# One hybrid gMLP/MLA step: the prompt tile's statistics on two engines, its keys last, and the eighth tile's rope queries turned during the attention

## The chip, the cores and the metric

One NeuronCore of a Trainium2 chip runs the whole program in one launch. The metric is device time in microseconds (us). Before the change three runs took 627.07, 629.03 and 629.16 us; the median is 629.03 us. Engines are called as in the profile: PE (TensorE), ACT (ScalarE), DVE (VectorE), POOL (GpSimd), SP (SyncE, which issues most of the DMAs).

## The reference

One layer over 1024 latent tokens and 128 prompt tokens, width 1024:

- h = rmsnorm(x) * (1 + scale) + shift, with scale and shift from a conditioning vector; z = h @ w_in, split into u, v, gate A (512 each), c_q (256), c_kv (128), k_rope (64), gate B (512).
- Group A mixes v over 128 positions and multiplies by gelu(u) and silu(gate A).
- Group B is latent attention with 4 heads: q = rmsnorm(c_q) @ w_uq gives per head 128 plain and 64 rope columns; ckv = rmsnorm(c_kv). The latent queries see all 1024 latent keys (rope turned by position) and 256 cached keys (queries and keys not turned) in one softmax; the prompt's 128 queries see the prompt's keys alone.
- y = concat(A, attention * silu(gate B)) @ w_o, x + gate * y, and a last rmsnorm. ckv and k_rope of the prompt are outputs too.

## The kernel before, in words

The 1152 tokens are nine tiles of 128: tiles 0 to 7 are latent, tile 8 (`NS`) is the prompt. Every large product is done in three float32r products of a high and a low part (`passes3`, L154): each PSUM result is copied rounded by ACT (the high part), and DVE subtracts that copy from the PSUM result (`lo_of`, L110, the low part). So a PE result comes back to PE by way of ACT and then DVE.

The text that the change touches is the stretch between the last input projection and the first heads of the attention:

1. **z tiles** (L1074 to L1088). For each tile t, 24 products (`z_chunk`, L1055) make c_q, c_kv and k_rope in one PSUM bank `zacc`. Between the chunks of tile t stand products for earlier tiles: `q_rope(t-2)`, `cq_transpose(t-1)`, `fold(t-1)`, `q_rope_T(t-3)` and some `q_nope`. `merged` (L211) puts them between the chunks by their cost numbers. After the last chunk, `z_stats` copies the bank to SBUF (`zs`), squares c_q and c_kv for their norms, takes roots, and scales the key (`kvn`).
2. **set-up** (L1089 to L1124). PE turns the keys (`keys`: `kT00`, `kT01` for tiles 0 to 3, `kT40`, `kT41` for 4 to 7, one for the plain, one for the rope part), the prompt's c_q (`cqT8`), the rope queries of tiles 6, 7 and 8 (`qrT`), makes the prompt's rope queries (`qr8`) and the plain queries of the third group of tiles (`qn20` to `qn23`), and turns the prompt's keys (`kT8`).
3. **attention**. A head (t, h) has three score steps on PE: two of five 128x512 products (`s1` banks, `lat`) and one of five 128x256 products (`s2`, `con`). DVE takes the row maximum, ACT the exponentials, DVE the reciprocal, POOL scales the 1280 columns (`e`). `value_steps` then turns `e` in five steps (`pT`, four transposes each), ACT copies each (`ph`), DVE makes the rest (`pl`), and PE multiplies with the values (`o`). The prompt's own small attention (`own_steps`) has four PE steps: scores, `pT8`, `o8`, and `at8` (L1401), the product with `wuv`. In pass c of the loop at L1472 the scores of heads 2c+2 and 2c+3 are merged with the values of the pair before.

The order is written by the program: `later(dt, fn)` puts an ACT, DVE or POOL instruction that much planned time behind its PE step, `run` adds the step's cost to the planned time, and `need` pulls forward what a step must have. Each engine then works through its list strictly in that order, whatever the real times are. Banks come from two pools: `pst` with 2 banks (tag `t`: `pT`, `at`, `cqT`, folds) and `psa` with 6 (tag `acc`, until the attention opens). A new tile in a pool waits until the last reader of the tile that had its bank is done: with two `pst` banks, the third `t` tile in a row waits for the readers of the first. `pss` and `pso`, which take `psa`'s banks, hold the scores and the outputs.

Of the kernel before, what the change touches and what calls it, by code (L numbers as in the profile page):

```python
# [18 lines left out]
P = 128  # L19
NT = 9  # L20
# [73 lines left out]
def tile_hymba_step(ctx: ExitStack, tc: tile.TileContext, I, O):  # L94
# [805 lines left out]
    def z_stats(t, ps):  # L900
# [9 lines left out]

        def scales():
# [41 lines left out]
        later(0.35, squares)  # L953
        later(0.9, rope_key)
        later(1.5, scales)

    def cq_transpose(t):
        last = t == NT - 1
        ps = (psa if last else pst).tile([P, 512], F32, tag="acc" if last else "t", name=f"cqT{t}")
        for q in range(2):  # L960
            T.transpose(ps[:, q * P : (q + 1) * P], zt[t][:, q * P : (q + 1) * P], ident)
        src = ps[:, 0:256].rearrange("p (q c) -> p q c", q=2)
        dh = cqh[:, :, t * P : (t + 1) * P]

        def low():
            lo_of(cql[:, :, t * P : (t + 1) * P], src, dh)
            made.add(("cq", t))

        later(0.4, lambda: S.copy(dh, src))
        later(0.85, low)  # L970
# [14 lines left out]
    rot = {}  # L985

    def q_rope(t):
# [4 lines left out]
        un = zp.tile([P, 4, 64], F32, tag="qun", name=f"qun{t}", bufs=3)  # L992
        rot[t] = [un]

        def raw():
            S.copy(un, ps[:, :256].rearrange("p (h r) -> p h r", h=4))
# [3 lines left out]
            r1 = zp.tile([P, 4, 64], F32, tag="qr1", name=f"qr1{t}", bufs=2)  # L1000
# [10 lines left out]
        later(0.85, raw)  # L1011

    def q_rope_T(t):
# [3 lines left out]
        late = t == NS  # L1017
# [19 lines left out]
    def keys(t0, n, kind):  # L1037
        need(*[("k", t0 + i) for i in range(n)])
        ps = (psa if t0 == 4 else pst).tile([P, 512], F32, tag="acc" if t0 == 4 else "t", name=f"kT{t0}{kind}")
        for i in range(n):  # L1040
            src = kvn[:, t0 + i, :] if kind == 0 else krd[:, t0 + i, :, :].rearrange("p a r -> p (a r)")
            T.transpose(ps[:, i * P : (i + 1) * P], src, ident)
        sl = slice(t0 * P, (t0 + n) * P)
        dh, dl = (kch, kcl) if kind == 0 else (krh, krl)
        later(0.11 * n + 0.1, lambda: S.copy(dh[:, sl], ps[:, : n * P]))
        later(0.25 * n + 0.3, lambda: lo_of(dl[:, sl], ps[:, : n * P], dh[:, sl]))
# [23 lines left out]
    with tc.manual_schedule(engines=engines):  # L1070
# [3 lines left out]
        for t in range(NT):  # L1074
# [3 lines left out]
            beside += [(1.05, lambda n=n: q_nope(*n)) for n in NOPES.get(t, [])[:1]]  # L1078
            if t >= 1:
                beside.append((0.25, lambda t=t: cq_transpose(t - 1)))  # L1080
            if 1 <= t < 5:
                beside.append((0.45, lambda t=t: fold(t - 1)))
            if t >= 3:
                beside.append((0.45, lambda t=t: q_rope_T(t - 3)))
            beside += [(1.05, lambda n=n: q_nope(*n)) for n in NOPES.get(t, [])[1:]]
            if t == NT - 1:
                beside.append((0.75, lambda: q_rope(t - 1)))
# [8 lines left out]
        vl = kv.tile([P, 11, P], F32R, tag="vl", name="vl")  # L1096
        for i, (dh, dl) in enumerate(((kch, kcl), (krh, krl))):
# [3 lines left out]
        later(11.0, lambda: pool_copy(cv[0], ctxr[:, 2, :]))  # L1101
        later(11.0, lambda: G.tensor_tensor(cv[1], ctxr[:, 2, :], f32(cv[0]), op=ALU.subtract))
        for t0, c in ((8, 1), (0, 4), (4, 4)):
            later(11.5, lambda t0=t0, c=c: values(t0, c))
        for cost, fn in (
# [336 lines left out]
    with tc.manual_schedule(engines=engines):  # L1442
# [29 lines left out]
        for c in range(len(pairs)):  # L1472
            sc = [s_ for i in (2 * c + LEAD, 2 * c + LEAD + 1) if i < len(heads) for s_ in score_steps(*heads[i])]
            if c == 0:
                sc = sc[:3] + own[1:2] + sc[3:5] + own[2:3] + sc[5:] + own[3:]
# [3 lines left out]
            if 2 * c + LEAD + 1 == 11:  # L1479
                c_wo, wo = opened("wo", side="left")  # L1480
# [211 lines left out]
```

## Time and profile before

| | us |
|---|---|
| three runs | 627.07, 629.03, 629.16 |
| profiled execution, its own time | 627.81 |
| its span, first to last instruction | 625.9 |
| mean granted TensorE clock | 0.995 of full |
| PE busy | 611.2 (98%) |
| DVE busy | 362.0 (58%) |
| ACT busy | 265.3 (42%) |
| POOL busy | 177.8 (28%) |

Stages of the span, read by the lines that run in them: start and first projections to about 131 us, channel products to 245, z tiles to 310, set-up to 321, attention to about 535, output projection to the end. Busy PE time counts matmuls with modelled ends, one laid over the next, so a start-to-start distance tells more than a duration. "[0.96 <-DVE cql L111]" behind an instruction says that its engine sat idle for 0.96 us before it and that the named instruction ended the wait.

### The profile page before, as it was taken

To read this page: it belongs to the slowest core of one execution; us is meant where nothing else is said; L and a number is where in the kernel's file an instruction comes from. 1 tells how busy PE (TensorE), PEld (TensorE's weight loads), DVE (VectorE), ACT (ScalarE), POOL (GpSimd) and SP (SyncE) were. 2 spreads that over 40 slices of the span, in tenths; PEclk is the share of its full clock that TensorE was granted. 3 is DMA by queue.
4 is the path that set the end of the run, shared out by engine and by line. 5 is a ranking of instruction groups with operands and counts; after the bars stand their busy time and mean duration, and the time that the engine had idled before them with its cause. 6 is when DMAs were issued, how large, how long until landed. Compare 5 with 4: busy or idle time off the path is not lost.

```text
span 625.9 us, 9804 instructions
## 1 busy us (share of the span) xinstructions
PE 611.2 (98%) x3703; PEld 555.2 (89%) x3703; DVE 362.0 (58%) x839; ACT 265.3 (42%) x638; POOL 177.8 (28%) x217
## 2 busy tenths in 40 slices
PE   7999999999999999999989999999999999999995
PEld 7678889999999999999977999999999988888884
DVE  4694466049555100456677656776666754487655
ACT  7556753112111111555666555555646543132212
POOL 2461223345445500433444212332222341000001
PEclk8999999999999999999999999999999999999999
DMA  8992010052331303000010000001101123423311
GB/s 318 389 374 69 1 34 2 2 181 70 117 110 55 93 8 110 27 2 1 1 41 1 2 0 2 1 2 35 35 1 34 35 69 107 163 101 135 111 57 67
DMA packets 15966, 46.32 MB, mean 74 GB/s; under 512 B 1952, under 2 KB 4912, under 8 KB 15920
## 3 DMA queue, kind: packets, MB, share of 16 engines
q1 hardware_dynamic: 15776, 45.51, 20.7%
q8 instruction: 29, 0.48, 0.3%
q10 hardware_dynamic: 144, 0.20, 0.1%
q14 instruction: 17, 0.14, 0.1%
HBM read 40.87 MB, written 4.83 MB: 73 GB/s over the span
## 4 chain that ended last, share of the span: by engine, by line
PE 92%; DVE 3%; ACT 2%; DMA 1%; issue 1%; SPq 0%; ACTq 0%; DVEq 0%
PE tp L746 6%; PE tp L159 6%; PE tp L157 6%; PE tp L158 6%; PE pT L1218 5%; PE w L1467 5%; PE w L1466 5%; PE w L1465 5%; PE o L1242 3%; PE o L1244 3%; PE o L1243 3%; PE s L1174 3%; PE s L1173 3%; PE s L1171 3%; PE s L1172 3%; PE s L1175 3%
## 5 line engine op out<-in xcount | busy, mean ns | idle before, releaser
L111 DVE TENSOR_TENSOR pl<-pT,ph 128x512 fp32r<-128x512 f32 x81 | 55.4, 686 | 48.1 <-ACT ph L1222 47.8
L1162 POOL TENSOR_SCALAR e<-e,rs 128x1280 f32<-128x1280 f32 x32 | 42.9, 1341 | 137.0 <-DVE rs L1161 118.3
L158 PE MATMUL tp<-area,w2h 128*128 128x384 f32 x216 | 72.6, 336 | 0.0
L159 PE MATMUL tp<-area,w2l 128*128 128x384 f32 x216 | 72.6, 336 | 0.0
L157 PE MATMUL tp<-area,w2h 128*128 128x384 f32 x216 | 72.6, 336 | 0.0
L1156 ACT ACTIVATE e<-s,nb,scl 128x256 f32<-128x256 f32 x64 | 56.0, 879 | 36.0 <-DVE nb L1150 35.9
L1222 ACT CAST ph<-pT 128x512 fp32r<-128x512 f32 x80 | 45.3, 588 | 43.5 <-PE pT L1218 40.7
L1218 PE MATMUL pT<-ident,e 128*128 128x128 f32 x320 | 47.9, 273 | 0.6 <-DVE pl L111 0.6
L1242 PE MATMUL o<-ph,vh 128*128 128x256 f32 x160 | 47.8, 299 | 0.0
L111 DVE TENSOR_TENSOR w2l<-w2r,w2h 128x1024 fp32r<-128x1024 f32 x12 | 19.9, 1654 | 45.1 <-POOL w2h L114 45.1
L1244 PE MATMUL o<-ph,vl 128*128 128x256 f32 x160 | 44.9, 281 | 0.0
L1243 PE MATMUL o<-pl,vh 128*128 128x256 f32 x160 | 44.8, 280 | 0.0
L1467 PE MATMUL w<-area,ml 128*128 128x512 f32 (+1 forms) x114 | 43.2, 379 | 0.0
L1218 PEld LDWEIGHTS pT<-ident,e 128*128 128x128 f32 x320 | 37.5, 140 | 4.3 <-DVE pl L111 1.5
L157 PEld LDWEIGHTS tp<-area,w2h 128*128 128x128 f32 x216 | 40.5, 188 | 0.6 <-issue 0.5
L158 PEld LDWEIGHTS tp<-area,w2h 128*128 128x128 f32 x216 | 40.5, 188 | 0.2
L159 PEld LDWEIGHTS tp<-area,w2l 128*128 128x128 f32 x216 | 40.5, 188 | 0.0
L1146 DVE TENSOR_REDUCE m<-s 128x1 f32<-128x1024 f32 x32 | 38.9, 1216 | 1.9 <-PE s L1175 1.9
L1171 PE MATMUL s<-kch,area 128*128 128x512 f32 (+2 forms) x100 | 38.9, 389 | 0.0
L746 PE MATMUL tp<-area,w2h 128*128 128x384 f32 x144 | 37.4, 340 | 0.0
L1174 PE MATMUL s<-krh,area 128*128 128x512 f32 (+2 forms) x100 | 35.4, 354 | 0.0
L1173 PE MATMUL s<-kch,area 128*128 128x512 f32 (+2 forms) x100 | 35.4, 354 | 0.0
(308 smaller groups left out, 1579.8 us busy)
## 6 DMA issues: line engine op xcount, KB each, us to landing
ada<-in_ada_ss SPq DMA_DIRECT2D x16, 512.0 KB, 10.3
w2r<-in_w_t SPq DMA_DIRECT2D x12, 512.0 KB, 3.7
x<-in_x SPq DMA_DIRECT2D x9, 512.0 KB, 5.9
xr<-in_x SPq DMA_DIRECT2D x9, 512.0 KB, 4.4
adag<-in_ada_g SPq DMA_DIRECT2D x8, 512.0 KB
wor<-in_w_o SPq DMA_DIRECT2D x8, 512.0 KB, 3.3
out_y<-y SPq DMA_DIRECT2D x8, 512.0 KB, 2.7
wvr<-in_w_v SPq DMA_DIRECT2D x8, 256.0 KB, 8.8
```

The lines of the kernel that those rows point to most:

```text
L111: V.tensor_tensor(lo, src, f32(hi), op=ALU.subtract)
L157: T.matmul(ps, wh, xh, start=j == 0, stop=False)
L158: T.matmul(ps, wh, xl, start=False, stop=False)
L159: T.matmul(ps, wl, xh, start=False, stop=j == n - 1)
L746: T.matmul(tps[i, g][:, :GW], w_[i][:, k, :], x_[k, g], start=k == 0 and j == 0, stop=k == NK - 1 and j == 2)
L1156: S.activation(e[:, sl], src, AF.Exp, bias=nb, scale=scl[:, t : t + 1], accum_out=su[:, i : i + 1])
L1171: T.matmul(ps, qh_, kch[:, sl], start=True, stop=False)
L1218: T.transpose(ps[:, w : w + P], es[t, h][:, c * P : (c + 1) * P], ident)
L1242: T.matmul(o, vh[:, kt, :], ph[:, sl], start=c == 0, stop=False)
L1243: T.matmul(o, vh[:, kt, :], pl[:, sl], start=False, stop=False)
L1244: T.matmul(o, vl[:, kt, :], ph[:, sl], start=False, stop=c == n - 1)
L1467: T.matmul(ps, b, woh[k][:, c0:c1], start=False, stop=k == NK - 1)
```

## The change: what it does

- In each z tile, `cq_transpose`, `fold` and `q_rope_T` are one step beside the chunks, not up to three. Tile 8's list gets `q_rope_T(6)`, which stood in the set-up.
- The evictions of tile 7's rope queries (`qun7`, `qr17` and POOL's three operations) come later (planned 3.4 behind the product, not 0.85), in a small SBUF pool of their own (`ra`), and `q_rope_T(7)` moves into pass c = 2 of the attention.
- The prompt's squares read the SBUF copy `zs`, not the PSUM bank: c_q's on DVE, c_kv's on ACT (`last_squares`); its roots and scales are planned later.
- The key banks of tiles 0 to 7 all come from `psa`. The prompt's rope and plain keys share one bank (`last_keys`) and stand behind `qrT8`; before, they were two tiles between the plain queries.
- `at8` moves from the end of pass c = 0 to behind the first score step of pass c = 1.

```diff
+        def last_squares(part):
+            j1 = sm.tile([P, 256], BF16, tag="j1", name=f"j1{t}", bufs=1)
+            if part == 0:
+                V.scalar_tensor_tensor(j1, zs[:, 0:256], 1.0, zs[:, 0:256], op0=ALU.mult, op1=ALU.mult, accum_out=ssz[:, 0:1])
+            else:
+                S.activation(j1[:, :128], zs[:, 256:384], AF.Square, accum_out=ssz[:, 1:2])
...
         later(0.3, lambda: S.copy(zs, ps[:, :448]))
-        later(0.35, squares)
+        if t == NS:
+            later(0.9, lambda: last_squares(0))
+            later(1.72, lambda: last_squares(1))
+        else:
+            later(0.35, squares)
         later(0.9, rope_key)
-        later(1.5, scales)
+        later(2.5 if t == NS else 1.5, scales)
...
-        later(0.4, lambda: S.copy(dh, src))
-        later(0.85, low)
+        later(0.05 if last else 0.4, lambda: S.copy(dh, src))
+        later(0.42 if last else 0.85, low)
...
         def raw():
+            home, tag, n = (zp, "qun", 3) if t < 7 else (aside[0], f"qun{t}", 1)
+            un = home.tile([P, 4, 64], F32, tag=tag, name=f"qun{t}", bufs=n)
...
-        later(0.85, raw)
+        later({7: 3.4, 8: 1.2}.get(t, 0.85), raw)
...
-        late = t == NS
+        late = t >= 7
         tp = (pst if late else psa).tile([P, 512], F32, tag="t" if late else "acc", name=f"qrT{t}")
...
-        ps = (psa if t0 == 4 else pst).tile([P, 512], F32, tag="acc" if t0 == 4 else "t", name=f"kT{t0}{kind}")
+        ps = (psa if t0 < 8 else pst).tile([P, 512], F32, tag="acc" if t0 < 8 else "t", name=f"kT{t0}{kind}")
...
+    def last_keys():
+
+        need(("k", NS))
+        ps = pst.tile([P, 512], F32, tag="t", name="kT8")
+        sl = slice(NS * P, NT * P)
+        for i, src in enumerate((krd[:, NS, :, :].rearrange("p a r -> p (a r)"), kvn[:, NS, :])):
+            T.transpose(ps[:, i * P : (i + 1) * P], src, ident)
+        for i, (dh, dl) in enumerate(((krh, krl), (kch, kcl))):
+            part = ps[:, i * P : (i + 1) * P]
+            later(0.2, lambda dh=dh, part=part: S.copy(dh[:, sl], part))
+            later(0.6, lambda dh=dh, dl=dl, part=part: lo_of(dl[:, sl], part, dh[:, sl]))
...
+            full = []
             if t >= 1:
-                beside.append((0.25, lambda t=t: cq_transpose(t - 1)))
+                full.append((0.25, lambda t=t: cq_transpose(t - 1)))
             if 1 <= t < 5:
-                beside.append((0.45, lambda t=t: fold(t - 1)))
+                full.append((0.45, lambda t=t: fold(t - 1)))
             if t >= 3:
-                beside.append((0.45, lambda t=t: q_rope_T(t - 3)))
+                full.append((0.45, lambda t=t: q_rope_T(t - 3)))
+            if full:
+                beside.append((sum(f[0] for f in full), lambda full=full: [f[1]() for f in full]))
...
             if t == NT - 1:
+                beside.append((0.45, lambda: q_rope_T(t - 2)))
                 beside.append((0.75, lambda: q_rope(t - 1)))
...
             (0.45, lambda: keys(4, 4, 1)),
-            (0.45, lambda: q_rope_T(6)),
-            (0.45, lambda: q_rope_T(7)),
             (0.75, lambda: q_rope(8)),
             (1.05, lambda: q_nope(2, 0)),
-            (0.15, lambda: keys(8, 1, 1)),
-            (0.15, lambda: keys(8, 1, 0)),
             (1.05, lambda: q_nope(2, 1)),
             (1.05, lambda: q_nope(2, 2)),
             (0.25, lambda: q_rope_T(8)),
+            (0.3, last_keys),
             (1.05, lambda: q_nope(2, 3)),
...
             if c == 0:
-                sc = sc[:3] + own[1:2] + sc[3:5] + own[2:3] + sc[5:] + own[3:]
+                sc = sc[:3] + own[1:2] + sc[3:5] + own[2:3] + sc[5:]
+            if c == 1:
+                sc = sc[:1] + own[3:] + sc[1:]
+            if c == 2:
+                sc = sc[:4] + [(0.45, lambda: q_rope_T(7))] + sc[4:]
```

ACT's list from the copy of the prompt's bank on, before (`z8` is `zs` of the prompt, `j18` the squares with their sums `ssz8`, `zw8` the roots, `kch`/`krh` the high parts of the plain and rope keys, `cqh` that of c_q):

```order
L952 COPY z8_3142<-zacc8_3040 128x448
L908 ACTIVATE j18_3162,ssz8_3143<-zacc8_3040 128x256
L909 ACTIVATE j18_3162,ssz8_3143<-zacc8_3040 128x128
L1045 CAST kch_3148<-kT00_3165 128x512
L918 ACTIVATE zw8_3183<-ssz8_3143,epsb_107 128x1 x2
L1045 CAST krh_3150<-kT01_3176 128x512
L969 CAST cqh_2354<-cqT8_3190 128x2x128
```

And the same stretch of ACT's list now:

```order
L959 COPY z8_3149<-zacc8_3040 128x448
L1059 CAST kch_3155<-kT00_3166 128x512
L980 CAST cqh_2354<-cqT8_3186 128x2x128
L1059 CAST krh_3157<-kT01_3179 128x512
L916 ACTIVATE j18_3191,ssz8_3150<-z8_3149 128x128
L1059 CAST kch_3155<-kT40_3193 128x512
L925 ACTIVATE zw8_3207<-ssz8_3150,epsb_107 128x1 x2
L1010 COPY qun7_3214<-qr7_3137 128x256
```

The copy of the prompt's c_q (`cqh`) now stands third, not seventh, and the roots and `qun7` stand behind two key banks.

PE's list at the turn from pass c = 0 to c = 1, before (`s110` is the score bank of tile 1, head 0; `pT00_0` and `pT00_1` are the first two steps of the first value pair):

```order
L1405 MATMUL at8_3480<-e8_3386,wuv_2364 128x128 x4
L1171 MATMUL s110_3489<-kch_3148,area0_117 128x512
L1172 MATMUL s110_3489<-kcl_3149,area0_117 128x512
L1173 MATMUL s110_3489<-kch_3148,area0_117 128x512
L1174 MATMUL s110_3489<-krh_3150,area0_117 128x512
L1175 MATMUL s110_3489<-krl_3151,area0_117 128x512
L1218 MATMUL pT00_0_3496<-ident_75,e00_3338 128x128
L1218 MATMUL pT00_0_3496<-ident_75,e01_3385 128x128
```

And now, from the end of the same score step on:

```order
L1205 MATMUL s110_3474<-krl_3158,area0_117 128x512
L1248 MATMUL pT00_0_3484<-ident_75,e00_3332 128x128
L1248 MATMUL pT00_0_3484<-ident_75,e01_3379 128x128
...
L1248 MATMUL pT00_1_3491<-ident_75,e00_3332 128x128
L1248 MATMUL pT00_1_3491<-ident_75,e01_3379 128x128
...
L1435 MATMUL at8_3499<-e8_3380,wuv_2364 128x128 x4
L1248 MATMUL pT00_2_3510<-ident_75,e00_3332 128x128
L1248 MATMUL pT00_2_3510<-ident_75,e01_3379 128x128
```

`at8` now stands behind two value steps, as the third `t` tile in a row, and a third value step stands behind it; the second half of `s110`'s scores, which stood before that third value step, now follows it.

DVE's list at the place in pass c = 2 where the tile 7 rope queries are turned, before (`pl01_2`, `pl01_3` are low parts of the second value pair, `mixB` takes `at00`, `rs12` is head (1, 2)'s reciprocal sum):

```order
L111 TENSOR_TENSOR pl01_2_3669<-pT01_2_3663,ph01_2_3668 128x512
L1263 TENSOR_TENSOR mixB_1379<-mixB_1379,at00_3694 128x2x128
L1160 TENSOR_TENSOR rs12_3648<-su12_3647 128x1
L1161 RECIPROCAL rs12_3648<-rs12_3648 128x1
L111 TENSOR_TENSOR pl01_3_3703<-pT01_3_3697,ph01_3_3702 128x512
```

And now:

```order
L111 TENSOR_TENSOR pl01_2_3668<-pT01_2_3662,ph01_2_3667 128x512
L1190 TENSOR_TENSOR rs12_3634<-su12_3633 128x1
L1191 RECIPROCAL rs12_3634<-rs12_3634 128x1
L1293 TENSOR_TENSOR mixB_1379<-mixB_1379,at00_3688 128x2x128
L111 TENSOR_TENSOR pl01_3_3697<-pT01_3_3691,ph01_3_3696 128x512
L1046 TENSOR_TENSOR area2_119<-qrT7_3702,area2_119 64x4x128 x2
```

The two small operations of `rs12`, which wait for head (1, 2)'s exponentials, now stand ahead of `mixB`; `qrT7`'s bank is the one that `mixB` reads from.

## Rows read from the trace of the kernel before

**Rows 1.** The page's busy time by engine: busy us, share of the span, instructions.

```profile
PE 611.2 (98%) x3703; PEld 555.2 (89%) x3703; DVE 362.0 (58%) x839; ACT 265.3 (42%) x638; POOL 177.8 (28%) x217
```

**Rows 2.** Windows: stretch, length, busy us (count) per engine, clock, DMA, GB/s.

```profile
245.00:310.00 65.00, 65.00 (x373) 60.77 (x372) 35.74 (x118) 34.76 (x104) 22.07 (x62) 1.00 0.04 10
```

**Rows 3.** Timeline of PE in the set-up: start, us, engine, line, operation, tiles.

```profile
309.58 0.37 PE L1064 MATMUL zacc<-qh,area 128*128 128x448 f32 x1
...
314.45 0.38 PE L159 MATMUL qr<-wrh,cql 128*128 128x256 f32 x1 [0.96 <-DVE cql L111]
...
315.02 0.34 PE L157 MATMUL qn<-cqh,wfh 128*128 128x384 f32 x1
...
316.07 0.27 PE L1042 MATMUL kT<-ident,krd 128*128 128x128 f32 x1
...
319.91 0.44 PE L1022 MATMUL qrT<-ident,qun 128*128 128x128 f32 x2 [1.15 <-DVE krl L111]
...
321.23 0.39 PE L1171 MATMUL s<-kch,area 128*128 128x512 f32 x1
```

**Rows 4.** Timeline of ACT in the set-up.

```profile
310.03 0.53 ACT L952 COPY z<-zacc 128x448 f32<-128x448 f32 x1 [0.23 <-PE zacc L1064]
...
311.23 0.58 ACT L1045 CAST kch<-kT 128x512 fp32r<-128x512 f32 x1
311.70 0.49 ACT L918 ACTIVATE zw<-ssz,epsb 128x1 f32<-128x1 f32 x2
...
315.94 0.37 ACT L996 COPY qun<-qr 128x256 f32<-128x256 f32 x1
```

**Rows 5.** Timeline of DVE in the set-up.

```profile
312.22 0.17 DVE L921 RECIPROCAL zr<-zw 128x2 f32<-128x2 f32 x1 [0.70 <-ACT zw L918]
...
313.99 0.41 DVE L111 TENSOR_TENSOR cql<-cqT,cqh 128x256 fp32r<-128x256 f32 x1
...
314.68 0.92 DVE L931 SCALAR_TENSOR_TENSOR kvn<-z,zr,kvg 128x128 f32<-128x128 f32 x1
```

**Rows 6.** Line L931 over the whole span: duration ns min/median/max, first and last start.

```profile
L931 DVE SCALAR_TENSOR_TENSOR kvn<-z,zr,kvg x9: 353/906/924, 254.6 to 314.7; 128x128 f32<-128x128 f32 x9
```

**Rows 7.** Timeline of PE at the turn from pass c = 0 to 1.

```profile
337.16 1.16 PE L1405 MATMUL at<-e,wuv 128*128 128x128 f32 x8 [0.44 <-ACT e L1396]
338.07 0.48 PE L1171 MATMUL s<-kch,area 128*128 128x512 f32 x1
...
339.31 1.03 PE L1218 MATMUL pT<-ident,e 128*128 128x128 f32 x8
...
341.92 0.66 PE L1218 MATMUL pT<-ident,e 128*128 128x128 f32 x4 [0.41 <-DVE pl L111]
```

**Rows 8.** Timeline of ACT at the same place.

```profile
339.38 1.19 ACT L1156 ACTIVATE e<-s,nb,scl 128x1024 f32<-128x1024 f32 x1
...
340.56 1.07 ACT L1222 CAST ph<-pT 128x512 fp32r<-128x512 f32 x2
```

**Rows 9.** Timeline of DVE at the same place.

```profile
341.17 1.29 DVE L111 TENSOR_TENSOR pl<-pT,ph 128x512 fp32r<-128x512 f32 x2
```

**Rows 10.** Timeline of PE in pass c = 2.

```profile
354.55 0.28 PE L1242 MATMUL o<-ph,vh 128*128 128x256 f32 x1
...
357.21 0.48 PE L1171 MATMUL s<-kch,area 128*128 128x512 f32 x1
```

**Rows 11.** Timeline of ACT in pass c = 2.

```profile
357.18 0.20 ACT L1156 ACTIVATION_READ_ACCUMULATOR e<-s,nb,scl 128x1 f32 x1
```

**Rows 12.** Timeline of DVE in pass c = 2.

```profile
357.06 0.42 DVE L1263 TENSOR_TENSOR mixB<-mixB,at 128x256 f32<-128x256 f32 x1 [0.95 <-PE at L1261]
357.48 0.16 DVE L1160 TENSOR_TENSOR rs<-su 128x1 f32<-128x1 f32 x1
```

**Rows 13.** Windows of the first 17 us (columns as in rows 2).

```profile
6.00:12.00 6.00, 4.26 (x43) 3.13 (x41) 3.21 (x10) 4.86 (x9) 1.60 (x1) 1.00 0.98 350
12.00:17.00 5.00, 4.89 (x24) 4.72 (x25) 4.21 (x8) 3.74 (x9) 1.27 (x1) 0.66 1.02 419
```

More of the change, by code (lines that the diff above doesn't have):

```diff
@@ L985, in tile_hymba_step @@
     rot = {}
+    aside = []
     def q_rope(t):
@@ L991, in q_rope @@
         passes3(ps[:, :256], [(cqh[:, q, sl], cql[:, q, sl], wrh[:, q, :], wrl[:, q, :]) for q in range(2)])
-        un = zp.tile([P, 4, 64], F32, tag="qun", name=f"qun{t}", bufs=3)
-        rot[t] = [un]
+        rot[t] = []
         def raw():
+            home, tag, n = (zp, "qun", 3) if t < 7 else (aside[0], f"qun{t}", 1)
+            un = home.tile([P, 4, 64], F32, tag=tag, name=f"qun{t}", bufs=n)
+            rot[t] = [un]
             S.copy(un, ps[:, :256].rearrange("p (h r) -> p h r", h=4))
@@ L999, in raw @@
                 return
-            r1 = zp.tile([P, 4, 64], F32, tag="qr1", name=f"qr1{t}", bufs=2)
+            r1 = (zp if t < 7 else aside[0]).tile([P, 4, 64], F32, tag="qr1", name=f"qr1{t}", bufs=2 if t < 7 else 1)
             r2 = zp.tile([P, 4, 64], F32, tag="qr2", name=f"qr2{t}", bufs=2)
@@ L1045, in keys @@
         later(0.11 * n + 0.1, lambda: S.copy(dh[:, sl], ps[:, : n * P]))
-        later(0.25 * n + 0.3, lambda: lo_of(dl[:, sl], ps[:, : n * P], dh[:, sl]))
+        later(0.85 if (t0, kind) == (0, 0) else 0.25 * n + 0.3, lambda: lo_of(dl[:, sl], ps[:, : n * P], dh[:, sl]))
+    def last_keys():
[8 more added lines that the diff above has]
+            later(0.6, lambda dh=dh, dl=dl, part=part: lo_of(dl[:, sl], part, dh[:, sl]))
     def values(t0, n):
@@ L1096, in tile_hymba_step @@
         vl = kv.tile([P, 11, P], F32R, tag="vl", name="vl")
+        c_ra, ra = opened("ra", side="left")
+        aside.append(ra)
         for i, (dh, dl) in enumerate(((kch, kcl), (krh, krl))):
@@ L1100, in tile_hymba_step @@
         cv = [v_[:, 9:, :].rearrange("p a r -> p (a r)") for v_ in (vh, vl)]
-        later(11.0, lambda: pool_copy(cv[0], ctxr[:, 2, :]))
-        later(11.0, lambda: G.tensor_tensor(cv[1], ctxr[:, 2, :], f32(cv[0]), op=ALU.subtract))
+        later(9.0, lambda: pool_copy(cv[0], ctxr[:, 2, :]))
+        later(9.0, lambda: G.tensor_tensor(cv[1], ctxr[:, 2, :], f32(cv[0]), op=ALU.subtract))
         for t0, c in ((8, 1), (0, 4), (4, 4)):
-            later(11.5, lambda t0=t0, c=c: values(t0, c))
+            later(9.5, lambda t0=t0, c=c: values(t0, c))
         for cost, fn in (
@@ L1479, in tile_hymba_step @@
             if 2 * c + LEAD + 1 == 11:
+                closed(c_ra)
                 c_wo, wo = opened("wo", side="left")
```

## The prediction

> **What bounds the kernel.** I read the page's busy time first, then the windows by stage, PE's waits, and PE's, ACT's and DVE's timelines where PE waits. PE is busy for 98% of the span [rows 1], and in the z tiles for all of 65 us [rows 2]: an edit counts there only if it takes work or a wait from PE. Waits are left in two places. In the set-up the prompt's rope queries wait 0.96 us for a low part on DVE, and the turning of its queries 1.15 us for a bank that DVE frees late [rows 3]. At the start of the attention `at8` waits 0.44 us and the third value step 0.41 us [rows 7]. More than some 4 us cannot be won, 0.6% of the time.
>
> The sum is made against the profiled execution: 627.81 us, its span of 625.9 and 1.9 around it. The median of the three runs, 629.03, lies 1.2 above; the change found is added to that median.
>
> **Grouping in the z tiles.** Transposes move to stand beside other transposes; number and form stay, and PE has no idle time there [rows 2]. I count nothing. The bound: a product straight behind transposes lasts 0.48 us, an undisturbed one of its kind 0.39 [rows 3, 7]. There are seven fewer such places (one each in tiles 1, 2 and 6, two in 3 and 4), so at best -0.6. The evictions that move are each used a tile later.
>
> **The set-up.** Times here count from the start of the last z product, 309.58; the attention's first product then stood at 11.65 (321.23) [rows 3]. One transpose is 0.11 (the eight passes of `at8` take 0.91, 337.16 to 338.07) [rows 7].
>
> Now: ACT copies the prompt's bank from 0.45 to 0.98 [rows 4]. DVE squares c_q from that copy, an operation the trace does not show. The nearest row is the scaling of the key, which also reads two SBUF tiles: 0.35 us at least, 0.91 in the median [rows 6]. I take 0.92, since POOL starts its copies of the prompt's rope key on the same signal; it ends at 1.95. One low part of 0.65 (1.29 for two) [rows 9] follows and frees the bank of `qr8` at 2.6. PE, with its last product (0.2), 16 + 2 transposes, would be there at 2.2. Then the low part of c_q, 0.41 [rows 5], ends at 3.0, and `qr8`'s third product goes; from there to the end of `qr8` it is 0.57 (314.45 to 315.02) [rows 3]: 3.6. Three `qn` of 1.05 (315.02 to 316.07) and three transposes put PE at 7.1 before the prompt's plain key.
>
> That key, `kvn`, comes by ACT and DVE. ACT has, behind the copy, three key banks of 0.58 less 0.1 of overlap each (311.23 to 311.70), the copy of c_q (about 0.37), the squares (about as long as the roots), the roots 0.49 and `qun7` 0.37 [rows 4]: near 4.0, some of it waiting for PE. DVE turns `qr7` (as long as c_q's low part): 4.4. From the reciprocal to `kvn` it was 2.46 (312.22 to 314.68) with c_q's low part between them, which is now done before [rows 5]: 2.05, so `kvn` runs from 6.45 to 7.35. PE waits 0.3, turns the key, makes `qn23`, and begins the attention at 8.55. `qrT6`, four transposes, went ahead of the last z product: 8.55 + 0.44 = 9.0, against 11.65. Of these 2.65 us, the four transposes of `qrT7` (0.44) only move into the attention. **Gain: 2.2 us.** Bounds: with 0.35 for both SBUF operations no wait is left, 3.1; if ACT's longer list or the eight low parts behind `kvn` on DVE (at 0.65 each they would end at 12.6, and the first head's maximum is due at 11.0) are late by a microsecond, 1.2.
>
> Rows 6 show two durations for one form of instruction. The Trainium skill (SBUF — State Buffer, "SBUF: two separate sides") says that a VectorE operation with two SBUF inputs and a GpSimd operation that reads SBUF hold a shared pair of ports in turn, each for its whole duration. By that rule the squares, moved from ACT to DVE, are a bad trade while POOL is busy; the trace agrees with its two durations. Without it the set-up would begin the attention half a microsecond sooner.
>
> **`at8` behind two value steps.** In the list `at8` is now the third `pst` tile in a row, so it waits for the readers of the first: ACT's copy and DVE's low part of `pT00_0`. Those come late whatever PE does: ACT works on head (0, 3)'s exponentials until 340.57 and starts the two copies at 340.56 [rows 8], DVE the low parts at 341.17 [rows 9], and before the third value step waited for just that low part until 341.92 [rows 7]. The lists of ACT, DVE and POOL up to there are the same, so the chain moves with the start of the attention and not with PE. PE now starts the score step where `at8` had started to wait (337.16 - 0.44 = 336.72), needs 1.24 for it (338.07 to 339.31) and 0.88 for eight transposes [rows 7], stands before `at8` at 338.84 and waits 3.1 us, until 341.92. Queued behind it are the third value step and the other half of the scores: all of PE. By 341.92 the kernel before had `at8` (0.91) and that half (1.24) behind it. **Loss: 2.15 us**; the third value step's own bank comes free under `at8`. Bounds: 1.1 if the chain runs a microsecond earlier, 2.6 if DVE begins the attention 0.5 late.
>
> **`qrT7` in pass c = 2.** Its bank is freed by `mixB`'s use of `at00` on DVE, which now stands behind head (1, 2)'s reciprocal, so behind its exponentials. They ended at 357.38 [rows 11], 2.83 after the score step that feeds them (354.55) [rows 10]. With two small operations of 0.16 and `mixB` 0.42 [rows 12], and the gaps, that is 3.65. PE from the same point: one value step (0.4), then what took 354.55 to 357.21 [rows 10]: 3.05. The wait is 0.6, and since a low part now stands between the head's two maxima, I take **0.8 us** (bounds 0 and 1.3). Before, `mixB` had no such wait.
>
> Nothing else is long: POOL's value splits end later but are needed only by the first `o` products, some 20 us on; SP's list is unchanged.
>
> Sum: -2.2 + 2.15 + 0.8 = +0.75, so 628.6 on the profiled scale and **629.8 us** on that of the median: no change that can be told. Less than 0.5% (3.1 us) counts as none, about what a measurement of this kernel can tell.
>
> **Rivals.**
>
> 1. *The clock falls at the new wait* (slower). In the first 12 us PE was busy for 4.26 of 6 us at full clock, and the next 5 us ran at a mean of 0.66 of it, between the two levels of 1.2 and 2.4 GHz [rows 13]: 0.34 x 5 = 1.7 us of full-speed work lost. At `at8` PE would stand still for 3.1 us between transposes. Against it: the waits of about 1 us in the set-up went by without a fall (the mean over the span is 0.995). It decides if PE's standing still there lets the clock fall as its first 12 us did. Time: 629.8 + 1.7 = 631.5; chance 0.22. The Trainium skill (TensorE: Matmul & The Clock Gate, "Part 1: The HAM clock gate") says that the gate follows how busy the engine has recently been and knows only two ratios; rows 13 agree with both. By it this rival would be the likelier of the two outcomes at `at8`, and the time 631.5.
> 2. *The new wait isn't there* (faster). If the low part of `pT00_0` came 3 us sooner, `at8` and the third value step would not wait: -2.2 - 0.44 - 0.41 + 0.8 = -2.25, so 626.8. For it: `at8` no longer waits for its own copy. Against it: rows 8 and 9, whose work stands ahead of that low part in the new lists too. Chance 0.13.
> 3. *DVE becomes the bound of the set-up.* Its list there grew by the squares, and `qr17` now stands in the middle of the key's chain. If `kvn` ends a microsecond later, 1.2 us are won, not 2.2, and the first maximum is late by as much, which lengthens the wait at `at8`: +2.0, so 631.8. Chance 0.15.
>
> **How the numbers follow.** The sum as worked has 0.5; its own bounds (-3.1 + 1.1 + 0 and -1.2 + 2.6 + 1.3) would span 627.0 to 631.7, most of it within 628.3 to 631.0. Rival 2 reaches below, 1 and 3 above; leaving out about 2 in 10, the range is 627.2 to 632.2. Faster by over 0.5% means under 625.9: 0.4 of rival 2, 0.05, and a little for the grouping: 0.06. Slower means over 632.2: a third of rival 1, 0.4 of rival 3: 0.14. Within: 0.80.
>
> **What would show it.** Right: the attention's first product starts 2.65 us earlier, near 318.6; `qr8` waits a few tenths, once; PE's longest wait of the attention, about 3 us, stands before `at8` with DVE `pl` as releaser; a wait of under a microsecond before `qrT7`, released by DVE `mixB`; the z tiles as long as before plus `qrT6`. Wrong: no wait over 1 us at `at8` (rival 2), a granted clock below full behind it (rival 1), or `kvn` over 8 us behind the last z product (rival 3).

## The result, and the profile after

Ten executions of the changed kernel have a median of 631.41 us (629.43 to 634.13), ten of the kernel before 628.98 (627.07 to 629.30). The ratio is 1.0047, with a 95% interval of 1.0031 to 1.0063: slower by 0.47%, some 3 us by the ratio and 2.4 by the medians. The forecast was 629.8, 0.75 over the kernel before; the measured median lies 1.6 above the forecast, in the range and within 0.5%. But the interval leaves out 1 and reaches to 0.63%: the change can be told, where the forecast said that it can't. The profiled execution took 631.14 us (span 629.4) against 627.81 (span 625.9), 3.33 more.

Cut at landmarks of PE, the two traces differ in five places. The landmarks are the first and the last z product, the first product of the attention, the first products of `at00` and of `at01`, and the last product of the program.

| us | before | after | difference | foreseen |
|---|---|---|---|---|
| start to first z product | 245.29 | 246.99 | +1.70 | 0 |
| z tiles | 64.29 | 64.73 | +0.44 | +0.44 (`qrT6`) |
| last z product to first of the attention | 11.65 | 8.30 | -3.35 | -3.09 |
| from there to `at00` (holds `at8`) | 35.18 | 37.36 | +2.18 | +2.15 |
| `at00` to `at01` (holds `qrT7`) | 12.01 | 14.11 | +2.10 | +1.24 |
| from there to the last product | 249.69 | 249.69 | 0 | 0 |

The sum is +3.07; of the 3.33 the other 0.26 lies outside these landmarks: the execution's own time, less the time from the span's start to the last product, is 9.70 before and 9.96 after. It belongs to the change, since it is 9.95 to 10.17 in all twelve profiles with the new set-up and 9.65 in the other one without; what makes it stays open. Up to the first z product PE, ACT, DVE and POOL run the same instructions in the same order in both traces, so the +1.70 comes from no edit.

By the page's busy time, as [rows 1], PE is busy for 0.9 us more in as many instructions, and a window over the z tiles, as [rows 2], shows PE without a gap:

```profile
PE 612.1 (97%) x3703; PEld 556.2 (88%) x3703; DVE 362.9 (58%) x841; ACT 264.4 (42%) x636; POOL 178.3 (28%) x217
```

```profile
247.00:312.00 65.00, 65.00 (x374) 60.85 (x374) 38.00 (x118) 34.88 (x105) 21.90 (x61) 1.00 0.04 10
```

The windows of the start, as [rows 13]; the last three columns are PE's granted clock, the DMA share and GB/s. No instruction in them is changed, and yet the clock is at half speed (1.2 GHz) for all of 12 to 17 us, where it was 0.66 before, and is back at full only within 17 to 20. By these windows the half speed cost 0.34 x 5 = 1.7 us of full-speed work before, and 0.50 x 5 + 0.30 x 3 = 3.4 after; the difference is what the start grew by:

```profile
6.00:12.00 6.00, 3.87 (x41) 2.92 (x40) 2.89 (x9) 4.42 (x8) 1.57 (x1) 1.00 1.01 349
12.00:17.00 5.00, 4.47 (x24) 4.21 (x21) 3.99 (x7) 3.25 (x8) 1.28 (x2) 0.50 1.02 418
17.00:20.00 3.00, 3.00 (x12) 2.35 (x12) 1.73 (x7) 1.33 (x3) 0.74 (x2) 0.70 1.04 416
```

PE in the set-up, as [rows 3]: no wait over 0.1 us is left but 0.22 us for `kvn`.

```profile
311.72 0.36 PE L1090 MATMUL zacc<-qh,area 128*128 128x448 f32 x1
...
314.46 0.31 PE L159 MATMUL qr<-wrh,cql 128*128 128x256 f32 x1
...
318.80 0.33 PE L1068 MATMUL kT<-ident,kvn 128*128 128x128 f32 x1 [0.22 <-DVE kvn L938]
...
320.02 0.39 PE L1201 MATMUL s<-kch,area 128*128 128x512 f32 x1
```

DVE there, as [rows 5, 6]. The squares took 0.48 us from their start to the end of the readout (312.81 to 313.29, one laid over the other), not 0.92, and `kvn` 0.44; yet a step on 128x2 elements, 0.17 in the median, took 0.68 and ended as an addition of 0.73 on POOL did (316.67 to 317.40):

```profile
312.81 0.47 DVE L914 SCALAR_TENSOR_TENSOR j<-z 128x256 bf16<-128x256 f32 x1
313.21 0.08 DVE L914 DVE_READ_ACCUMULATOR j<-z 128x1 f32 x1
...
316.75 0.68 DVE L930 SCALAR_TENSOR_TENSOR zt<-zt,zv 128x2 f32<-128x2 f32 x1
...
318.31 0.44 DVE L938 SCALAR_TENSOR_TENSOR kvn<-z,zr,kvg 128x128 f32<-128x128 f32 x1
```

Beside the squares it was POOL's second copy of the rope key that took longer, 0.44 us, where the first took 0.24:

```profile
312.93 0.44 POOL L957 COPY krd<-z 128x64 f32<-128x64 f32 x1
```

The trace of before does have a row of the form of the squares, in the last stage, and it would have been the nearer one; 0.43 us (ns min/median/max in the row):

```profile
L1559 DVE SCALAR_TENSOR_TENSOR jf<-y x1: 426/426/426, 619.3 to 619.3; 128x256 bf16<-128x256 f32 x1
```

PE at the turn, as [rows 7], then ACT and DVE there, as [rows 8, 9]. `at8` waits 2.93 us for the low part of `pT00_0`, which DVE starts at 340.01; the half step of scores, before done ahead of that, follows at 342.11:

```profile
336.79 1.04 PE L1248 MATMUL pT<-ident,e 128*128 128x128 f32 x8
340.75 1.16 PE L1435 MATMUL at<-e,wuv 128*128 128x128 f32 x8 [2.93 <-DVE pl L111]
341.75 0.60 PE L1248 MATMUL pT<-ident,e 128*128 128x128 f32 x4
342.11 0.48 PE L1201 MATMUL s<-kch,area 128*128 128x512 f32 x1
```

```profile
339.40 1.07 ACT L1252 CAST ph<-pT 128x512 fp32r<-128x512 f32 x2
```

```profile
340.01 0.69 DVE L111 TENSOR_TENSOR pl<-pT,ph 128x512 fp32r<-128x512 f32 x1 [2.44 <-ACT ph L1252]
```

PE in pass c = 2, as [rows 10], then ACT and DVE, as [rows 11, 12]. Besides the wait of 1.05 before `qrT7` there is a second one, of 0.18, in the next pass: `qrT7`'s copies (ACT, 1.17) and low parts (DVE, 1.39) stand ahead of the next head's maximum, which starts only at 362.80, and the exponentials, copies and low part of the next value step follow it. Both waits count from a modelled end. From start to start the gap before `qrT7` is 1.3 us (the fourth transpose ahead of it starts at 357.83 + 3 x 0.11 = 358.16), 1.2 more than between two transposes.

```profile
357.83 0.60 PE L1248 MATMUL pT<-ident,e 128*128 128x128 f32 x4
359.47 0.44 PE L1036 MATMUL qrT<-ident,qr 128*128 128x128 f32 x2 [1.05 <-DVE mixB L1293]
...
368.52 0.66 PE L1248 MATMUL pT<-ident,e 128*128 128x128 f32 x4 [0.18 <-DVE rs L1190]
```

```profile
360.17 1.17 ACT L1045 CAST area<-qrT 64x512 fp32r<-64x512 f32 x2 [1.05 <-PE qrT L1036]
```

```profile
359.02 0.40 DVE L1293 TENSOR_TENSOR mixB<-mixB,at 128x256 f32<-128x256 f32 x1
...
361.37 1.39 DVE L1046 TENSOR_TENSOR area<-qrT,area 64x512 fp32r<-64x512 f32 x2 [1.35 <-ACT area L1045]
362.80 1.23 DVE L1176 TENSOR_REDUCE m<-s 128x1 f32<-128x1024 f32 x1
```

### The profile page after: what moved, and what is told of

Its sections match the earlier page's. It is cut to its first block, busy times and chain, and to the rows that moved or that the text cites. A ratio compares the mean times of both kernels' runs of the same rounds, so it can differ in the third digit from the quotient of the medians.

```text
span 629.4 us, 9804 instructions
## 1 busy us (share of the span) xinstructions
PE 612.1 (97%) x3703; PEld 556.2 (88%) x3703; DVE 362.9 (58%) x841; ACT 264.4 (42%) x636; POOL 178.3 (28%) x217
## 4 chain that ended last, share of the span: by engine, by line
PE 89%; DVE 4%; ACT 3%; DMA 1%; issue 1%; SPq 0%; ACTq 0%; DVEq 0%
PE tp L746 6%; PE tp L158 6%; PE tp L157 6%; PE tp L159 6%; PE w L1497 5%; PE w L1495 5%; PE w L1496 5%; PE pT L1248 5%; PE o L1272 3%; PE o L1274 3%; PE s L1203 3%; PE s L1204 3%; PE o L1273 3%; PE s L1202 3%; PE s L1201 3%; PE s L1205 2%
```

## The experiments

Twelve kernels ran, in three lots of four; beside each lot ran 22 to 31 executions of the kernel before. The table cuts one profiled execution of each at the same landmarks. Where nothing differs, the stages repeat to within 0.1 us; the start alone spreads over 3 us. The last column is the measured ratio to the kernel before.

| kernel | start | set-up | to `at00` | to `at01` | first z to last product | ratio (95%) |
|---|---|---|---|---|---|---|
| before | 245.29 | 11.65 | 35.18 | 12.01 | 372.82 | |
| after | 246.99 | 8.30 | 37.36 | 14.11 | 374.19 | 1.0047 (1.0031 to 1.0063) |
| at8_back | 245.62 | 8.31 | 35.24 | 14.03 | 372.00 | 0.9983 (0.9971 to 0.9995) |
| at8_other_bank | 245.49 | 8.33 | 37.94 | 14.09 | 374.77 | 1.0017 (1.0002 to 1.0031) |
| qrT7_apart | 246.70 | 8.33 | 37.34 | 14.44 | 374.53 | 1.0061 (1.0040 to 1.0083) |
| both_mended | 245.36 | 8.31 | 35.25 | 14.44 | 372.41 | 0.9998 (0.9986 to 1.0009) |
| qrT7_first | 247.24 | 8.33 | 35.60 | 12.01 | 370.34 | 0.9957 (0.9942 to 0.9971) |
| qrT7_setup | 245.39 | 8.32 | 36.85 | 12.00 | 371.59 | 0.9985 (0.9972 to 0.9997) |
| shift_one_input | 247.42 | 8.33 | 38.08 | 14.32 | 375.21 | 1.0030 (1.0017 to 1.0044) |
| qrT7_first_old_squares | 245.01 | 8.71 | 35.61 | 12.01 | 370.74 | 0.9972 (0.9959 to 0.9985) |
| first_and_shift | 245.07 | 8.32 | 34.78 | 12.01 | 369.58 | 0.9948 (0.9932 to 0.9963) |
| first_shift_long_warm | 247.96 | 8.30 | 34.81 | 12.00 | 369.58 | 0.9968 (0.9957 to 0.9978) |
| changed_long_warm | 246.37 | 8.30 | 40.22 | 14.06 | 376.99 | 1.0065 (1.0047 to 1.0084) |
| before_long_warm | 245.66 | 11.68 | 35.22 | 12.00 | 372.88 | 1.0013 (1.0001 to 1.0025) |

**at8_back.**

```diff
-                sc = sc[:3] + own[1:2] + sc[3:5] + own[2:3] + sc[5:]
-            if c == 1:
-                sc = sc[:1] + own[3:] + sc[1:]
+                sc = sc[:3] + own[1:2] + sc[3:5] + own[2:3] + sc[5:] + own[3:]
```

> The changed kernel with at8 put back to the end of pass c = 0; all else stays. Theory (at8 waits in a bank for the low part of pT00_0 and keeps the third value step and half a head of scores behind it): the stretch from the half score step to the third value step gives back 2.1 us; at8 waits under 0.5 us for its own copy on ACT, the third value step about 0.4 us for DVE's low part. 631.4 - 2.1 = 629.3 us. Rival (the low part of pT00_0 sets the end whatever stands before it, so the wait only goes over from at8 to the third value step): that step waits about 3 us and the time stays at 631.4.

The stretch to `at00` is 2.12 us shorter, and only the waits of before are left there, 0.43 us before `at8` and 0.41 before the third value step. The theory holds. By the ratios, 0.9983 and 1.0047, it is 4 us below the changed kernel, nearly twice that stretch. The rest can be the clock behind the long wait, which falls in some of the profiles below; in how many executions of the changed kernel it fell is not known.

**at8_other_bank.**

```diff
-            ps = pst.tile([P, 512], F32, tag="t", name="at8")
+            ps = pso.tile([P, 512], F32, tag="o", name="at8")
```

> The changed kernel with at8 at its new place, but in the bank that held o8, not in one of the two banks of the value transposes. Theory (two costs: the bank makes at8 wait, and the half head of scores stays behind the low part of pT00_0): at8 starts right behind the eight transposes, the next value step then waits 2.0 to 2.3 us for DVE's low part, and only at8's own 0.9 us is won: 630.5 us. Rival A (the bank is the whole cost): no wait above 0.5 us, 2.1 us won, 629.3. Rival B (the place, not the bank): nothing won, 631.4.

`at8` starts at once, and the next value step waits 2.04 us for DVE (the profile names the operation right behind the low part). Counted from the eight transposes that value step starts at 3.97 us (339.23 - 335.26), in the changed kernel at 4.96 (341.75 - 336.79): 0.99 is won, as the theory has it, and both rivals fall. But in this execution the clock fell behind the wait, so that 37.94 us is longer than 37.36. PE, and a window behind the wait:

```profile
335.26 1.03 PE L1248 MATMUL pT<-ident,e 128*128 128x128 f32 x8
336.13 1.06 PE L1435 MATMUL at<-e,wuv 128*128 128x128 f32 x8
339.23 0.66 PE L1248 MATMUL pT<-ident,e 128*128 128x128 f32 x4 [2.04 <-DVE rs L1190]
```

```profile
341.00:343.00 2.00, 2.00 (x11) 1.98 (x11) 1.47 (x2) 0.00 (x0) 0.00 (x0) 0.50 0.03 8
```

**qrT7_apart** and **both_mended** (the latter with `at8` back as well).

```diff
-                sc = sc[:4] + [(0.45, lambda: q_rope_T(7))] + sc[4:]
+                sc = sc + [(0.45, lambda: q_rope_T(7))]
```

> The changed kernel with qrT7 at the end of pass c = 2, behind a value step and a score step, where the last tile of its bank has long been read; the four transposes and the four evictions (1.17 us on ACT, 1.39 us on DVE) stay. Theory (its cost is the wait for mixB and what its evictions then hold up in the middle of a head's maxima): no wait over 0.2 us at qrT7, and the 2.1 us of that stretch fall to the transposes' 0.4: 631.4 - 1.7 = 629.7 us. Rival (the evictions hold up a head's softmax wherever they stand): only the wait before qrT7 goes and another of about a microsecond comes up in the pass after it: 630.9 to 631.2.

> The changed kernel with at8 back at the end of pass c = 0 and qrT7 at the end of pass c = 2. What is left of the change is the grouping in the z tiles, the new set-up and qrT7 in the attention. Theory (the 1.7 us that the changed kernel lost in its first 20 us is a matter of chance between executions, and the set-up gains 2.9 us less 0.4 for qrT7): 2.4 us under the kernel before, 626.6 where that one has 629.0. Rival (the start-up's loss belongs to the changed kernel): 1.4 us under it at most, 627.6, or the full 1.7 lost, 628.3; the mean clock of its runs then stays below that of the kernel before.

The wait before `qrT7` is gone and the stretch is no shorter: 14.44 us. The theory of the place falls. Its rival has the outcome right, another wait in the pass after, at 1.85 us larger than it gave; but that wait is for `qrT7`'s bank, not for a softmax. PE and DVE of qrT7_apart:

```profile
361.57 0.38 PE L1036 MATMUL qrT<-ident,qr 128*128 128x128 f32 x2
...
366.31 0.63 PE L1248 MATMUL pT<-ident,e 128*128 128x128 f32 x4 [1.85 <-DVE area L1046]
```

```profile
364.77 1.39 DVE L1046 TENSOR_TENSOR area<-qrT,area 64x512 fp32r<-64x512 f32 x2 [2.43 <-ACT area L1045]
```

`qrT7` holds its bank from 361.57 until DVE's second low part ends near 366.2, and the second value step behind it needs that bank. ACT's copies came only at 363.58, behind a head's exponentials. So both_mended stands 0.41 below the kernel before from the first z product on, not 2.4, and its ratio is 0.9998. The mean clocks of its executions, 0.990 to 0.997, are those of the kernel before, and its start took 245.36: the start's loss is no part of the change.

**qrT7_first** and **qrT7_setup** (both with `at8` back, and without the line of pass c = 2).

```diff
-        merged(first[:4] + own[:1] + first[4:], [])
+        merged(first[:2] + [(0.45, lambda: q_rope_T(7))] + first[2:4] + own[:1] + first[4:], [])
```

```diff
-        late = t >= 7
+        late = t >= NS
...
+            (0.45, lambda: q_rope_T(7)),
             (0.25, lambda: q_rope_T(8)),
```

> The changed kernel with at8 back at the end of pass c = 0, and qrT7 in the first head of the attention, behind its two halves of the scores, where no value transposes use its two banks yet and ACT and DVE wait for work (ACT 2.10 us before the first exponentials, DVE 2.12 before the prompt's maximum, in the changed kernel's trace). Theory (the 1.7 us that qrT7 lost in the value passes beside its transposes are its evictions, in the way of banks and of a head's softmax): the set-up's gain of 2.9 us stays but for the 0.4 us of transposes, with no new wait of over 0.2 us: 2.45 under the kernel before, 625.8 where that one has 628.2. Rival (its two low parts, 1.39 us on DVE, put the whole row of maxima late and the third value step waits for it): 1.5 under, 626.7.

> The changed kernel with at8 back at the end of pass c = 0 and qrT7 in the set-up, ahead of the prompt's rope queries, in one of the six banks there. Theory: 1.39 us of low parts come on DVE ahead of the first head's maximum, which had 0.41 us of slack there; the maximum is 1.0 us late, 0.55 beyond the 0.44 by which the attention starts later, and the third value step waits 0.95 us instead of 0.4: 1.9 us under the kernel before, 626.3 where that one has 628.2. Rival (the slack of the first heads takes it up): 2.45 under, 625.8.

In the first head the transposes cost 0.42 us (35.18 to 35.60) and nothing else: 372.82 to 370.34 is -2.48, forecast -2.45. In the set-up they cost 1.25 more than in the first head (36.85 to 35.60): 1.23 under the kernel before, where the theory had 1.9 and the rival 2.45. The theory's direction holds, but not its reason, a late maximum: the first head's third score step already waits, for DVE's last low part of the set-up. PE of qrT7_setup:

```profile
322.26 0.39 PE L1202 MATMUL s<-kch,area 128*128 128x256 f32 x1 [1.39 <-DVE area L111]
```

**qrT7_first_old_squares.**

```diff
-        if t == NS:
-            later(0.9, lambda: last_squares(0))
-            later(1.72, lambda: last_squares(1))
-        else:
-            later(0.35, squares)
+        later(0.35, squares)
...
-        later(2.5 if t == NS else 1.5, scales)
+        later(1.5, scales)
```

> As the kernel with qrT7 in the first head, but with the prompt's squares as before the change: both on ACT from the bank, at once, and the scales at their old due time; the order of the keys and queries stays new. Theory (the copy on ACT, the squares ahead of the keys' copies and the late low part for qr8 are what the squares' part of the change took away): qr8 waits 0.7 to 1.0 us again, the rest of the set-up's gain stays: 0.9 us over the kernel with the new squares. Rival (the order of the keys alone makes the gain): the same time as with the new squares, within 0.2 us. Rival B (the squares are the whole gain): 2.4 over, as the kernel before.

The set-up is 0.38 us longer, with 0.64 of wait before `qr8`; that lies between the theory (0.9) and the first rival (0.2), and rival B is out. So the squares are worth 0.4 of the set-up's gain, and its other edits together the rest: the order of keys and queries, the banks, and planned times, of which two (`kT00`'s low part and POOL's value splits, both earlier) are not in the diff of the change. They were not taken apart. The medians, 626.93 and 625.97, differ by more than the 0.40 from the first z product on; from one execution to the next the start moves by more than that. PE of qrT7_first_old_squares:

```profile
312.83 0.35 PE L157 MATMUL qr<-wrh,cqh 128*128 128x256 f32 x1 [0.64 <-DVE zv L926]
```

**shift_one_input** and **first_and_shift** (qrT7_first with the same line).

```diff
-            V.scalar_tensor_tensor(nb, m[:, 0:1], m[:, 1:2], nscl[:, t : t + 1], op0=ALU.max, op1=ALU.mult)
+            V.tensor_scalar(nb, m[:, 0:1], m[:, 1:2], nscl[:, t : t + 1], op0=ALU.max, op1=ALU.mult)
```

> The changed kernel with the softmax's shift nb (128x1) as an operation with one tensor and two per-partition scalars, in place of one with two tensors from SBUF; the value is the same. In the changed kernel the shift of head (0, 2) took 1.17 us where others took 0.22, from 332.42 to 333.59, when GpSimd's scaling of 1.35 us ended; the exponentials behind it waited 1.44. Theory (the two engines shut each other out there, and the chain from that shift to the low part of pT00_0 sets at8's wait): the shift takes about 0.2, at8's wait falls from 2.9 to 1.9 to 2.1, and the time by 0.9: near 629.2, where the changed kernel as it is should come to 630.1 beside a kernel before of 628.2. Rival A (the form of the instruction makes no difference: the shift waits as long): 630.1. Rival B (the chain is held elsewhere: the shift is short and at8's wait as long): 630.1.

> The kernel with qrT7 in the first head, at8 at the end of pass c = 0, and also the shift with one tensor and two per-partition scalars. Theory (the shift of head (0, 2) no longer waits for GpSimd, so the exponentials, the copy for at8 and the low part of pT00_0 all come 0.85 us sooner, as where the shift alone was changed): the waits of 0.42 us before at8 and 0.42 before the third value step go: 0.8 us less than with qrT7 in the first head alone, 3.3 under the kernel before, 625.3 where that one has 628.6. Rival (the shift, 0.27 us instead of 0.22 for each of 32 heads, costs in the steady part what it wins at the start): no gain, 626.1.

The shift's line over the whole span (ns min/median/max), of the changed kernel and of shift_one_input:

```profile
L1180 DVE SCALAR_TENSOR_TENSOR nb<-m,nscl x32: 219/220/1173, 324.1 to 508.6; 128x1 f32<-128x1 f32 x32
```

```profile
L1180 DVE TENSOR_SCALAR nb<-m,nscl x32: 272/273/274, 324.5 to 510.0; 128x1 f32<-128x1 f32 x32
```

The long one is gone, and `at8` starts 19.87 us behind the attention's first product instead of 20.73, 0.86 sooner; rivals A and B fall. The wait before it is 2.55 us, not the 1.9 to 2.1 of the theory: PE too came there sooner, by 0.5. In the profiled execution the gain did not reach the time, since the clock fell behind the wait here too; the median, 630.56, is 1.9 over that of the kernel before (628.65). In first_and_shift there is no long wait, and the theory is met to 0.1: 369.58 is 3.24 under the kernel before, with 0.15 left before the third value step. At a median of 624.76 us and a ratio of 0.9948 it is the fastest of all.

**first_shift_long_warm** (first_and_shift with the edit below), **changed_long_warm** and **before_long_warm** (`WARM0` counts PE's products ahead of its first real work).

```diff
-WARM0 = 24
+WARM0 = 28
```

> As that kernel, with 28 instead of 24 products ahead of the first real work on TensorE. In the executions profiled so far the wait for the first piece of in_ada_ss was 0.39 to 2.0 us, the granted clock behind it 1.00 where the wait was shortest and 0.50 to 0.66 where it was 0.78 and more, and the vision projections' end (the first z product) moved by as much as 2 us between executions. Theory (that wait and the fall of the clock behind it are the spread between executions, and the four products fill the wait): the clock stays full from 12 to 17 us, and nearly all executions are as short as the shortest without: 624.3 to 624.8. Rival (the products only put the first real work off): 625.3 to 626.0 as without.

> The changed kernel, otherwise as it is, with 28 instead of 24 products ahead of the first real work. Theory (of the 2.4 to 3 us that it was slower 1.4 to 1.7 is the change, the rest a worse draw in the start-up; and behind the 2.9 us at at8 the clock falls in some executions): 1.4 to 1.7 us over the kernel before with the same 28 products in its undisturbed executions, 629.2; some executions 1.5 us longer, at a lower mean clock. Rival (all of it is the change): 2.4 to 3 over.

> The kernel before with 28 instead of 24 products ahead of the first real work, as the measure for the changed kernel with as many. Theory (the spread between its executions is the start-up's clock): nearly all executions at 627.2 to 628.0, none of those near 629.4 that make up half of them without. Rival (the spread comes from elsewhere): two groups as without, median 628.2 to 629.

The clock is full from 12 to 17 us in all three, and yet the first z product comes no sooner (245.66 to 247.96). In first_shift_long_warm, the latest, the clock fell later; its windows:

```profile
12.00:17.00 5.00, 4.31 (x27) 3.32 (x28) 4.23 (x8) 4.32 (x10) 1.27 (x1) 1.00 1.02 415
17.00:20.00 3.00, 2.44 (x26) 1.24 (x24) 1.71 (x8) 1.52 (x2) 0.00 (x0) 1.00 1.03 411
20.00:25.00 5.00, 3.59 (x29) 2.20 (x29) 3.38 (x4) 3.60 (x7) 3.77 (x4) 0.81 0.98 352
```

The kernel before became no faster (629.10, 628.19 to 630.35): the theory of the longer warm-up falls. changed_long_warm is 632.92, 3.8 over before_long_warm, not 1.4 to 1.7. Its profiled execution (633.33) shows why: PE and the windows at `at8`, where the wait is the same 2.93 us as in the changed kernel, and `at8` takes 2.08 us instead of 1.16:

```profile
340.09 2.08 PE L1435 MATMUL at<-e,wuv 128*128 128x128 f32 x8 [2.93 <-DVE pl L111]
```

```profile
337.00:339.00 2.00, 0.17 (x2) 0.00 (x0) 0.00 (x0) 2.00 (x5) 0.00 (x0) 1.00 0.00 0
339.00:341.00 2.00, 0.91 (x4) 0.91 (x5) 1.51 (x4) 0.80 (x2) 0.54 (x1) 0.62 0.00 0
341.00:343.00 2.00, 2.00 (x11) 2.00 (x11) 0.69 (x1) 0.00 (x0) 0.79 (x1) 0.50 0.04 8
343.00:345.00 2.00, 2.00 (x7) 1.52 (x6) 0.69 (x1) 0.59 (x1) 0.00 (x0) 0.50 0.00 0
345.00:347.00 2.00, 2.00 (x14) 2.00 (x13) 1.22 (x1) 0.03 (x1) 0.00 (x0) 0.67 0.00 0
```

The stretch to `at00` is 40.22 us, 2.86 longer than without the fall. The same 8 us in the changed kernel, where the clock stayed at full, in at8_other_bank, in shift_one_input and in this one; the mean granted clock is the last column but two:

```profile
339.00:347.00 8.00, 6.25 (x44) 5.81 (x45) 5.27 (x10) 3.63 (x9) 1.34 (x1) 1.00 0.01 2
```

```profile
339.00:347.00 8.00, 7.77 (x42) 7.20 (x43) 4.68 (x10) 3.08 (x7) 1.35 (x1) 0.79 0.01 2
```

```profile
339.00:347.00 8.00, 6.66 (x36) 6.26 (x37) 4.63 (x9) 2.22 (x5) 1.34 (x1) 0.79 0.01 2
```

```profile
339.00:347.00 8.00, 6.91 (x30) 6.43 (x31) 4.11 (x7) 1.41 (x4) 1.33 (x1) 0.57 0.01 2
```

## Why the prediction was right or wrong

**The range held, the sum was short by a term, and one rival came true in some executions.** The change itself is +1.37 us from the first z product to the last product of the program in the profiled executions, +1.63 with the 0.26 behind it, where the sum had +0.75. That the median, 631.41, stands beside rival 1's 631.5 is in part luck: in the profiled execution (631.14) the clock did not fall at `at8`, and 1.70 of its time came from the start, which no term had.

- *Grouping, 0.* Right: the z tiles grow by 0.44 us, the price of `qrT6`'s four transposes (the two were not run apart).
- *The set-up, -2.65 with the transposes moved.* Right in size, measured -2.91 (+0.44 - 3.35). The squares were priced too high, by 0.44: the hold-up by POOL that the price had in it did not come, and a row of their form was there to read (0.43). `qr8`, foreseen to wait a few tenths, did not, and PE waited 0.22 for `kvn`, which ran from 6.59 to 7.03 behind the last z product (6.45 to 7.35 foreseen): rival 3 is out.
- *`at8`, +2.15.* Right in the profiled execution, +2.18, for the reason given: at8_back takes all of it away, and at8_other_bank splits it into the bank (0.99) and the scores left behind the chain. Rival 2 is out.
- *`qrT7`, "I take 0.8 us (bounds 0 and 1.3)".* This is the term that was wrong. The stretch grew by 2.10, of which 0.42 are the transposes in qrT7_first: 1.68, over the bound. Some 1.2 of it is the wait ahead of `qrT7` (from start to start; the releaser is the foreseen `mixB`), 0.4 over the estimate. The other 0.4 to 0.5 the prediction did not count, what `qrT7` issues: two copies on ACT and two low parts on DVE, 2.56 us in all, in a pass where the banks turn over by just these engines. They stand ahead of a head's maximum and, in qrT7_apart, hold the bank itself; in the first head, where these engines wait for work, the whole 1.68 is gone.
- *Rival 1, the clock at `at8`.* Not in the profiled execution, where it stayed full after 2.93 us of waiting, nor in qrT7_apart (2.92), but shown in three other kernels: at8_other_bank (2.04 of wait), shift_one_input (2.55) and changed_long_warm (2.93), at half speed behind it. Its price was 1.6 in the first two (37.94 and 38.08, where 0.99 and 0.86 less than 37.36 were due) and 2.86 in the third, where the mean clock of the 8 us is 0.57, not 0.79; 1.7 was set. None of the nine profiles without that wait shows a fall there. With three falls in five profiles the chance of 0.22 looks too low, and it is not one outcome for a kernel but can differ between executions.
- *The start, left out.* The first z product lies between 245.01 and 247.96 us in the fourteen profiles, without a changed instruction ahead of it but for the four warm products in three. In the eleven others it goes with the clock: 245.01 to 245.62 where the clock is at full from 12 to 17 us or, with no later start, at half for a part of that, 246.70 to 247.24 where it is at half for all of it, and 247.42 in shift_one_input, where it fell twice. PE's wait for its first real operand was up to 0.9 us in the first group and 1.6 to 2.0 in the second; which of the two makes the other, no run here takes apart. The kernel before ran in two groups by itself: in the last lot twelve of 22 executions at 627.27 to 628.26, ten at 628.99 to 630.35, nine of these at a mean clock of 0.990 or 0.991. So 1.70 of the 3.33 between the two profiled executions is this draw, and the profile of before was from the faster group.

The 2.4 us between the medians lie between the change's +1.37 without a fall and its +4.17 with one (376.99 - 372.82). The fastest of the ten executions, 629.43 at a mean clock of 0.998, is what the profile of before and the change give without either draw: 627.81 + 1.63 = 629.44. Which of the others had a fall at `at8`, which a bad start, their mean clocks (0.985 to 0.992) don't tell apart; that stays open.

## What to carry to other kernels

A step that moves takes its evictions along: price the bank it holds until the last reader and the queue behind each eviction, not only the wait ahead of it, and put it where those engines wait for work (0.42 us there, 2.1 in a full pass). Where one engine is busy for nearly all of the span, a new stall of 2 to 3 us may cost up to its length again, since the clock may fall behind it (1.6 us behind 2.04 and 2.55, 2.86 behind 2.93; nothing in two other profiles). And compare kernels by landmarks within the trace: stages repeated to 0.1 us where whole executions differed by 3.

## What the runs showed of the hardware

- One wait, two outcomes: behind 2.93 us without work on PE the granted clock stayed at 1.00 (2.4 GHz) in the changed kernel's profile and went to 0.50 (1.2 GHz) in that of changed_long_warm. The Trainium skill (TensorE: Matmul & The Clock Gate, "Part 1: The HAM clock gate") has the ratio follow how busy the engine has recently been, and only two ratios; the runs agree with both, and no run here shows what decides at one and the same wait.
- A VectorE operation on 128x1 elements, 0.22 us in the median, lasted until a GpSimd operation beside it ended, at 333.59; with one tensor and two per-partition scalars it took 0.27 in each of 32, at this place too, in the middle of the same GpSimd operation. DVE and POOL of the changed kernel, then of shift_one_input:

```profile
332.42 1.17 DVE L1180 SCALAR_TENSOR_TENSOR nb<-m,nscl 128x1 f32<-128x1 f32 x1
```

```profile
332.24 1.35 POOL L1192 TENSOR_SCALAR e<-e,rs 128x1280 f32<-128x1280 f32 x1 [1.40 <-ACT ph L1409]
```

```profile
332.84 0.27 DVE L1180 TENSOR_SCALAR nb<-m,nscl 128x1 f32<-128x1 f32 x1
```

```profile
332.66 1.34 POOL L1192 TENSOR_SCALAR e<-e,rs 128x1280 f32<-128x1280 f32 x1 [1.40 <-ACT ph L1409]
```

The Trainium skill (SBUF — State Buffer, "SBUF: two separate sides") has VectorE operations with two SBUF inputs wait out a GpSimd operation that reads SBUF and started first; the trace agrees at this place, and the form with scalars did not wait.
